# Clears of operand rings moved behind the first weight loads in a hybrid decoder layer

## The chip, the cores and the metric

The kernel runs on one core of a Trainium2 chip. The metric is device microseconds for one execution, as the median of several runs. The core has five engines with queues of their own, each worked off in order: TensorE (PE in the profile), VectorE (DVE), ScalarE (ACT), GpSimd (POOL) and SyncE (SP), which here only issues transfers. Engines wait for each other, and for transfers, by semaphores.

## The reference

One decoder layer over 1024 prompt tokens and 8 decode tokens, model width 1024, then a final norm. What is computed, cut to what matters here:

```
h = rmsnorm(x, norm1_g);  proj = h @ w_in            # 18 tiles of 128 columns
# columns 0..511: pooling mixer (windows 2, 4, 8, 16); columns 512..: RWKV-7
r, k, v, zw, za, zg = split(token_shift(proj[:, 512:]))
decay = exp(-exp(-softplus(-(w0 + tanh(zw) @ w_lora_up)) - 0.5))
a = sigmoid(a0 + za @ a_lora_up);  g = sigmoid(zg) @ g_lora_up
# per token and head: S = S * decay + (S @ -kk) (kk * a)^T + v k^T;  y = S @ r
x = x + concat(pool_out, rwkv_out) @ w_out
x = x + square(relu(rmsnorm(x, norm2_g) @ w_up)) @ w_down
y = rmsnorm(x, norm_f_g)
```

## The kernel before

All matrix products are done in three passes: an operand is split into a rounded half (`h`) and the rest (`l`), and `gemm` (L169 to L177) adds `h*h`, `h*l` and `l*h`. For a weight tile, `weights` (L147) loads `wr` over GpSimd's queue, ScalarE writes the rounded half `wh` (through `act`, L92) and VectorE the rest `wl` (L165). The ring of `wr` has four buffers. A tile of 128 output columns has two such loads of 256 KB, each with four of its eight 128-row pieces.

The start of the program is what matters here. `token_block(0)` and `token_block(1)` load the first two blocks of 256 tokens over SP's queue (`xr`, L213), round them (`xh` on ScalarE, `xl` on VectorE, L217), and sum their squares (`acc`, eight squares on ScalarE); a matmul with ones gives the sum over channels (`ss`, L239), and `rstd` (L130) makes the scale `rs` of it: `ms`, `tt`, `rs` on ScalarE, three steps on VectorE. Projection tiles 16 and 17 (`pj16`, `pj17`) come first: they hold the low-rank inputs `zw`, `za` and `zg`. `low_rank` (L305) scales them by `rs` (`pr`, L284), mixes in the shifted token (`z`) and takes the tanh and sigmoid in several steps on ScalarE and VectorE (`sigm`). Then `rkv` projects tiles 8, 4 and 12 (`pj8`, `pj4`, `pj12`) for the first head pair. A projection writes one of two shared PSUM buffers, and `pj17` two others, so the four blocks of `pj16` and `pj17` can be done before `rs` is known.

Later, `stage1` (L337) writes scaled operands into the buffers `ARs`, `RBs` and `BK`, of which half must be zero, and `inverse` (L455) writes the `TTs`. These buffers are cleared once. In the kernel before, `ARs`, `RBs` and `BK` are cleared on GpSimd where they are made (L434), and `TTs` on VectorE in `inverse_setup` (L445 to L453), which is called behind the first token blocks and the loads of weight tiles 16 and 17.

The order on each engine isn't that of the source: the framework's scheduler places each instruction by its priority, which follows the order of the source, and by its own estimate of when an operand is ready. `tc.high_priority` moves a step ahead. So the clears at L434, which stand ahead in the source, also stand ahead in GpSimd's queue.

Of the kernel before, what the change touches and what calls it, by code (L numbers as in the profile page):

```python
# [79 lines left out]
def build(nc, tc, I, O, dbg=None):  # L80
    with ExitStack() as ctx:
        _build(ctx, nc, tc, I, O, dbg or {})


def _build(ctx, nc, tc, I, O, dbg):
    V, A, PE, SY, GP = nc.vector, nc.scalar, nc.tensor, nc.sync, nc.gpsimd
# [342 lines left out]
    ARs = [rcp.tile([P, 4, 2, 2, 64], F32, name=f"AR{i}") for i in range(NSEG)]  # L429
    RBs = [rcp.tile([P, 4, 2, 64], F32, name=f"RB{i}") for i in range(NSEG)]  # L430
    BK = rcp.tile([P, 4, 4, 64], F32, name="BK")
    ring = [0]
    for t in (*ARs, *RBs, BK):
        GP.memset(t, 0.0)  # L434

# [2 lines left out]
    TTs = [rcp.tile([P, 8, 2, 64], F32, name=f"TT{i}") for i in range(2)]  # L440
# [4 lines left out]
    def inverse_setup():  # L445
        V.memset(Xs, 0.0)
        for t in range(16):
            V.memset(Xs[:, 17 * t:17 * t + 1], 1.0)
        V.memset(Es, 0.0)
        for t in TTs:  # L450
            V.memset(t, 0.0)
        for d in inv_d:
            SY.dma_start(d[:, :, 16:32, 32:64].rearrange("c g i k -> (c g) i k"), Es[0:32, :, 0:32])  # L453

# [331 lines left out]
    for w, r, src in ((wup, R[0], "w_lora_up"), (aup, R[1], "a_lora_up")):  # L786
# [4 lines left out]
        V.tensor_tensor(lol[r], raw[r], f32(w[r]), op=ALU.subtract)  # L791
    SY.dma_start(glu, I["g_lora_up"])
    inverse_setup()
    low_rank(0)

# [272 lines left out]
```

## Time and profile before

| | |
|---|---|
| median of 3 runs | 1366.24 us (1365.65 to 1368.66) |
| profiled execution | 1369.13 us, span 1367.4 us |
| TensorE busy | 1306.5 us, 96% |
| VectorE, ScalarE, GpSimd busy | 829.6, 592.7, 156.5 us |
| first matmul | 13.71 us after the span's start |

The profile shows one execution, with times from the start of its span. A row of the timeline gives the start, the duration, the engine, the line, the operation, and in brackets how long the engine had stood idle and what released it. Where several instructions are merged (x4), the duration is from the first one's start to the last one's end. The chain of waits follows the work that ended last back to the start of the program.

### The profile page before, as it was taken

The page shows a single profiled execution, that of the slowest core. Times are in us where ns is not written, and L with a number is a line of the kernel's source. Part 1 is how long each engine was busy: PE and PEld are TensorE (multiplying, and loading weights), DVE is VectorE, ACT ScalarE, POOL GpSimd, SP SyncE. Part 2 cuts the span into 40 slices and gives each one's busy share as a digit, 9 for nine tenths or more (in the row PEclk, how much of TensorE's full clock was granted, in tenths as well). Part 3 has the DMA queues.
Part 4 walks back from the last instruction along what each step waited for, and adds up shares of the span by engine and source line. Part 5 has one row for each costly group of instructions (what it writes and reads, how often), then busy time and mean ns, then how long its engine had stood idle before and what let it go on. Part 6 is the DMA issues. An engine that isn't in the chain of part 4 may idle for free.

```text
span 1367.4 us, 24591 instructions
## 1 busy us (share of the span) xinstructions
PE 1306.5 (96%) x9844; PEld 1158.8 (85%) x9844; DVE 829.6 (61%) x1832; ACT 592.7 (43%) x1466; POOL 156.5 (11%) x306
## 2 busy tenths in 40 slices
PE   5999999999999999999999999999999999999996
PEld 5987778788777777798999999999999999999986
DVE  8887677778778656748644435445444354453447
ACT  7768777877777758526211212112111121121123
POOL 4101000210010021120010100100000100000000
PEclk9999999899999989999999999999999999999998
DMA  6323123222221244531111111111111111111103
GB/s 199 97 55 89 39 47 83 100 96 54 59 63 42 67 152 147 167 125 59 47 54 39 55 47 39 55 40 47 55 40 54 47 46 48 45 48 48 47 7 124
DMA packets 75315, 94.82 MB, mean 69 GB/s; under 512 B 46168, under 2 KB 52440, under 8 KB 75192
## 3 DMA queue, kind: packets, MB, share of 16 engines
q0 software_dynamic: 20480, 66.04, 15.1%
q1 hardware_dynamic: 53392, 25.36, 7.1%
q10 hardware_dynamic: 1328, 1.85, 0.4%
q8 instruction: 77, 1.26, 0.4%
q14 instruction: 38, 0.31, 0.1%
HBM read 79.67 MB, written 13.78 MB: 68 GB/s over the span
## 4 chain that ended last, share of the span: by engine, by line
PE 75%; ACT 9%; DVE 9%; DMA 3%; issue 2%; POOL 1%; SPq 0%; DVEq 0%; POOLq 0%; ACTq 0%
PE dn L175 26%; PE up L175 26%; PE pj L175 7%; PE mx L175 5%; ACT SV L92 2%; DVE tm L496 1%; PE sc L403 1%; PE pcs L580 1%; ACT Es L92 1%; ACT TT L92 1%; PE pcs L577 1%; DVE SV L589 1%; ACT wh L92 1%; PE pcs L573 1%; PE bkt L417 1%
## 5 line engine op out<-in xcount | busy, mean ns | idle before, releaser
L92 ACT ACTIVATE wh<-wr 128x512 fp32r<-128x512 f32 x230 | 143.8, 626 | 353.4 <-PE dn L175 276.2
L175 PE MATMUL up<-h2h,wl 128*128 128x260 f32 (+1 forms) x768 | 245.8, 320 | 0.0
L175 PE MATMUL up<-h2h,wh 128*128 128x260 f32 (+1 forms) x768 | 245.2, 320 | 0.5 <-DVE u L910 0.5
L175 PE MATMUL up<-h2l,wh 128*128 128x260 f32 (+1 forms) x768 | 245.0, 320 | 0.0
L175 PE MATMUL dn<-uh,wl 128*128 128x512 f32 (+1 forms) x720 | 231.2, 321 | 0.0
L175 PE MATMUL dn<-ul,wh 128*128 128x512 f32 (+1 forms) x720 | 230.8, 321 | 0.0
L175 PE MATMUL dn<-uh,wh 128*128 128x512 f32 (+1 forms) x720 | 230.5, 320 | 0.0
L949 DVE TENSOR_TENSOR x<-dn,x 128x260 f32<-128x260 f32 (+1 forms) x192 | 99.1, 516 | 189.8 <-PE dn L175 189.8
L175 PE MATMUL pj<-xh,wh 128*128 128x256 f32 (+1 forms) x576 | 175.3, 304 | 13.9 <-ACT wh L92 13.7
L165 DVE TENSOR_TENSOR wl<-wr,wh 128x512 fp32r<-128x512 f32 x230 | 156.5, 684 | 44.6 <-ACT wh L92 37.8
L175 PE MATMUL pj<-xh,wl 128*128 128x256 f32 (+1 forms) x576 | 171.0, 297 | 0.2 <-DVE wl L165 0.2
L175 PE MATMUL pj<-xl,wh 128*128 128x256 f32 (+1 forms) x576 | 170.5, 296 | 0.0
L175 PEld LDWEIGHTS up<-h2l,wh 128*128 128x128 f32 x768 | 144.6, 188 | 12.1 <-DVE h2l L892 0.4
L175 PEld LDWEIGHTS up<-h2h,wh 128*128 128x128 f32 x768 | 144.3, 188 | 11.6 <-DVE u L910 0.9
L175 PEld LDWEIGHTS up<-h2h,wl 128*128 128x128 f32 x768 | 144.6, 188 | 11.0
L92 ACT ACTIVATE uh<-u 128x260 fp32r<-128x260 f32 (+1 forms) x96 | 47.2, 492 | 238.6 <-DVE u L911 238.6
L175 PEld LDWEIGHTS dn<-ul,wh 128*128 128x128 f32 x720 | 135.6, 188 | 10.9 <-issue 0.2
L175 PEld LDWEIGHTS dn<-uh,wh 128*128 128x128 f32 x720 | 135.8, 189 | 10.4
L175 PEld LDWEIGHTS dn<-uh,wl 128*128 128x128 f32 x720 | 135.5, 188 | 10.6 <-issue 0.2
L175 PEld LDWEIGHTS pj<-xh,wh 128*128 128x128 f32 x576 | 111.4, 193 | 17.4 <-ACT wh L92 13.7
L910 DVE SCALAR_TENSOR_TENSOR u<-up,rs 128x260 f32<-128x260 f32 (+1 forms) x96 | 49.5, 517 | 120.9 <-PE up L175 114.3
L175 PEld LDWEIGHTS pj<-xl,wh 128*128 128x128 f32 x576 | 111.2, 193 | 2.4 <-issue 1.9
(295 smaller groups left out, 2224.3 us busy)
## 6 DMA issues: line engine op xcount, KB each, us to landing
wr<-in_w_in POOLq DMA_DIRECT2D x72, 256.0 KB, 3.1
wr<-in_w_up POOLq DMA_DIRECT2D x64, 256.0 KB, 2.8
wr<-in_w_down POOLq DMA_DIRECT2D x64, 256.0 KB, 2.9
wr<-in_w_out POOLq DMA_DIRECT2D x26, 256.0 KB, 3.1
xr<-in_xT SPq DMA_DIRECT2D x16, 256.0 KB, 3.7
mr<-mix SPq DMA_DIRECT2D x8, 260.0 KB, 3.5
x<-in_xT SPq DMA_DIRECT2D x2, 1040.0 KB, 9.1
blk<-AA SPq DMA_DIRECT2D x16, 128.0 KB, 3.3
```

Source lines behind the costliest of these rows:

```text
L92: A.activation(out, in_, func, bias=bias, scale=scale, **k)
L165: V.tensor_tensor(l[:, :w], raw[:, :w], f32(h[:, :w]), op=ALU.subtract)
L175: PE.matmul(ps, lhs, rhs, start=i == 0, stop=i == n - 1)
L403: PE.matmul(psc[:, c, :], BK[:, c, 2 * h:2 * h + 2, :], AR[:, c, :, h, :], start=True, stop=True)
L417: PE.transpose(pt[:, c, :], BK[:, c, 2 * h:2 * h + 2, :].rearrange("p a t -> p (a t)"), ident)
L496: V.tensor_tensor(pr[:, q], l[:, q].unsqueeze(2).to_broadcast([64, m, m, m]), r[:, q].rearrange("p k j -> p j k").unsqueeze(1).to_broadcas ...
L573: PE.matmul(pq, AR[:, c, 0, :, :], SV[:, c, :, :], start=True, stop=True)
L577: PE.matmul(pa, TT[:, g, :, :], Q, start=True, stop=True)
L580: PE.matmul(pu, BKT[:, c, :, :], SV[:, c, :, :], start=True, stop=True)
L589: V.scalar_tensor_tensor(dst, pu[R[h], h, :], U.gam[R[h], g:g + 1], sg[R[h], h, :], ALU.mult, ALU.add)
L910: V.scalar_tensor_tensor(u, ps[:, :n], 0.0, rs2[:, cs], ALU.max, ALU.mult)
L949: V.tensor_tensor(d, ps[:, :n], d, op=ALU.add)
```

## The change

The clears of `ARs`, `RBs` and `BK` are taken from where the buffers are made and put into `inverse_setup`, together with those of the two `TTs`, which move from VectorE to GpSimd. Nothing else in the source differs.

```diff
     BK = rcp.tile([P, 4, 4, 64], F32, name="BK")
     ring = [0]
-    for t in (*ARs, *RBs, BK):
-        GP.memset(t, 0.0)
...
         V.memset(Es, 0.0)
-        for t in TTs:
-            V.memset(t, 0.0)
+        for t in (BK, *ARs, *RBs, *TTs):
+            GP.memset(t, 0.0)
         for d in inv_d:
```

GpSimd's queue in the kernel before, from the last two of its nine clears (`wr` is a weight load; `SV` and `AA` are two small clears of the first head pair):

```order
L434 MEMSET RB_145 128x512
L434 MEMSET BK 128x1024
L157 DMA wr<-in_w_in 128x512 x4
L559 MEMSET SV_0_743 64x64 x2
L342 MEMSET AA_0_679 128x16
```

The same queue in the changed kernel, from the last of the framework's own constants:

```order
L1036 MEMSET const-uint8-127 128x1
L1040 UNCONDITIONAL_BRANCH
L157 DMA wr<-in_w_in 128x512 x4
L449 MEMSET BK 128x1024
L449 MEMSET AR_138 128x1024
```

The four loads of weight tiles 16 and 17 now stand at the head of the queue, and eleven clears behind them.

ScalarE's first steps in the kernel before (`xh0` is the rounded half of the first token block, two steps for each loaded `xr0`):

```order
L100 ACT_TABLE_LOAD
L92 ACTIVATE xh0_172<-xr0_0_176,vec_87 128x256 x2
L92 ACTIVATE xh0_172<-xr0_2_182,vec_87 128x256 x2
L92 ACTIVATE xh0_172<-xr0_4_194,vec_87 128x256 x2
L92 ACTIVATE xh0_172<-xr0_6_200,vec_87 128x256 x2
```

and in the changed kernel:

```order
L100 ACT_TABLE_LOAD
L92 ACTIVATE wh_159<-wr_157 128x512
L92 ACTIVATE xh0_163<-xr0_0_167,vec_87 128x256 x2
L92 ACTIVATE xh0_163<-xr0_2_173,vec_87 128x256 x2
L92 ACTIVATE wh_181<-wr_179 128x512
L92 ACTIVATE xh0_163<-xr0_4_185,vec_87 128x256 x2
```

The rounding of the first weight tile's two halves, which came behind 15 of the 16 roundings of `x`, now stands first and sixth.

ScalarE in the low-rank block of the kernel before. `z00` and `z10` are the two low-rank tiles of the first half of the tokens, `pr12` and `pr13` the scaled projections, `za0` a rounded half; `wh_461` and `wh_467` are the two halves of weight tile 8, for `pj8`, the projection behind `pj17`:

```order
L92 ACTIVATE z00_317<-pr12_1_376,ona_94 128x256
L92 ACTIVATE z10_320<-pr13_0_407,ona_94 128x256
L92 ACTIVATE carry_127<-pr13_0_407 128x1
L92 ACTIVATE wh_461<-wr_459 128x512
L92 ACTIVATE carry_127<-pr12_1_376 128x1
L92 ACTIVATE z00_317<-z00_317 64x512
L92 ACTIVATE za0_319<-z00_317 64x512
L92 ACTIVATE wh_467<-wr_465 128x512
```

The same place in the changed kernel, up to two steps behind `wh_461` (one more `z10` step and then `wh_467` follow):

```order
L92 ACTIVATE carry_127<-pr13_0_407 128x1
L92 ACTIVATE z10_320<-pr13_1_437,ona_94 128x256
L92 ACTIVATE carry_127<-pr12_1_376 128x1
L92 ACTIVATE z00_317<-z00_317 64x512
L92 ACTIVATE za0_319<-z00_317 64x512
L92 ACTIVATE carry_127<-pr13_1_437 128x1
L92 ACTIVATE z00_317<-z00_317 64x512
L92 ACTIVATE z10_320<-z10_320 128x512
L92 ACTIVATE z00_317<-z00_317 64x512
L92 ACTIVATE wh_461<-wr_459 128x512
L92 ACTIVATE z10_320<-z10_320 128x512
L92 ACTIVATE zw0_318<-z00_317 64x512
```

Between the `carry` of `pr13_0` and `wh_461` there was nothing; now eight steps of the low-rank block stand there. Ahead of these rows, the rounding `aup` of the second lora weight has moved from ahead of `ms` of the first token block to behind it. On TensorE the order differs only up to the end of `pj8` (16 rows), where in the kernel before four matmuls of its second token block stand within the first; behind that TensorE, and a little later the other engines too, have the same order in both kernels.

## Rows read from the trace of the kernel before

**Rows 1.** The page's busy times, their share of the span and instruction counts.
```profile
PE 1306.5 (96%) x9844; PEld 1158.8 (85%) x9844; DVE 829.6 (61%) x1832; ACT 592.7 (43%) x1466; POOL 156.5 (11%) x306
```
**Rows 2.** Chain of waits, 0 to 50 us: start us, us, what.
```profile
7.09 5.91 DMA wr<-in_w_in
...
13.71 7.62 PE pj L175 x42
...
29.21 0.70 DVE wl L165
...
29.95 17.29 PE pj L175 x142
```
**Rows 3.** Timeline of GpSimd, first 8 us: start us, us, what.
```profile
0.74 3.67 POOL L434 MEMSET AR<- 128x1024 f32 x4 [0.29 <-POOLq L1038]
4.35 1.91 POOL L434 MEMSET RB<- 128x512 f32 x4
6.20 0.96 POOL L434 MEMSET BK<- 128x1024 f32 x1
7.09 2.29 POOL L157 DMA_DIRECT2D wr<-in_w_in  x4
```
**Rows 4.** Tile views of wr (0 to 40 us) and of xr (0 to 25).
```profile
DMA to landing us min/median/max: 2.8/3.3/6.5
...
DMA to landing us min/median/max: 2.7/4.4/5.2
```
**Rows 5.** Busy by stretch (PE, PEld, DVE, ACT, POOL), PEclk, DMA share, GB/s.
```profile
1.00:2.00 1.00, 0.00 (x0) 0.00 (x0) 0.89 (x2) 1.00 (x1) 1.00 (x2) 1.00 0.15 32
...
10.00:13.00 3.00, 0.00 (x0) 0.00 (x0) 1.22 (x4) 0.70 (x2) 0.43 (x1) 1.00 1.03 373
```
**Rows 6.** Timeline of ScalarE, 0 to 33 us.
```profile
6.21 4.50 ACT L92 ACTIVATE xh<-xr,vec 128x256 fp32r<-128x256 f32 x11 [0.52 <-DMA xr<-in_xT]
...
18.24 1.66 ACT L92 ACTIVATE xr<-xr 128x512 f32<-128x512 f32 x3
...
22.23 0.48 ACT L92 ACTIVATE ms<-ss,sm 128x256 f32<-128x256 f32 x1 [0.70 <-PE ss L239]
...
28.56 0.62 ACT L92 ACTIVATE wh<-wr 128x512 fp32r<-128x512 f32 x1
...
29.17 0.62 ACT L92 ACTIVATE z<-z 64x512 f32<-64x512 f32 x1
29.82 0.63 ACT L92 ACTIVATE za<-z 64x512 fp32r<-64x512 f32 x1
30.47 0.63 ACT L92 ACTIVATE wh<-wr 128x512 fp32r<-128x512 f32 x1
```
**Rows 7.** Timeline of VectorE, 0 to 52 us.
```profile
2.46 1.03 DVE L125 TENSOR_SCALAR ona<-vec 128x14 f32<-128x14 f32 x1 [0.24 <-DMA vec<-in_vecs]
...
4.53 1.68 DVE L217 SCALAR_TENSOR_TENSOR xl<-xr,vec,xh 128x256 fp32r<-128x256 f32 x4
6.75 4.48 DVE L217 SCALAR_TENSOR_TENSOR xl<-xr,vec,xh 128x256 fp32r<-128x256 f32 x11 [0.54 <-ACT xh L92]
...
16.18 0.91 DVE L451 MEMSET TT<- 128x1024 f32 x1 [0.16 <-issue]
...
31.32 0.69 DVE L165 TENSOR_TENSOR wl<-wr,wh 128x512 fp32r<-128x512 f32 x1
```
**Rows 8.** Timeline of TensorE, 18 to 20 us.
```profile
18.44 0.42 PE L175 MATMUL pj<-xh,wl 128*128 128x256 f32 x1
18.66 0.42 PE L175 MATMUL pj<-xh,wh 128*128 128x256 f32 x1
...
19.03 0.28 PE L175 MATMUL pj<-xh,wl 128*128 128x256 f32 x1
```
**Rows 9.** TensorE by stretch: busy us (matmuls), granted clock, DMA share, GB/s.
```profile
234.00:237.40 3.40, 2.20 (x91) 1.00 0.51 171
237.40:240.80 3.40, 3.40 (x45) 0.50 0.02 5
```

## The prediction

> **What bounds the kernel now.** I read the page's engine rows first: TensorE is busy for 96% of the span [rows 1], so a change pays only where TensorE stands still, or where it is made to. Then the chain of waits over the first 50 us [rows 2]: until 13.71 us it isn't on TensorE at all. GpSimd clears nine buffers [rows 3], issues the first weight load at 7.09, the load lands 5.91 us later, ScalarE rounds it, and only then does the first projection start. From 13.71 to 47.24 TensorE is all but continuous (7.62 us of matmuls, the square sums, then 142 matmuls in 17.29 us [rows 2]). One more view decides this case: what ScalarE does between 22 and 33 us [rows 6], because the chain comes back to it, through the `wl` at 29.21 [rows 2], just when TensorE has run out of prepared work: its matmul with that `wl` starts at 29.95, 0.04 us after the `wl` is done.
>
> **The change, step by step.**
>
> *The first four weight loads* move from 7.09 to where the clears began, 0.74 [rows 3]: 6.35 us earlier. How long will one take there? The trace has no weight load at the start. Loads of this size landed 2.8 us after issue at best and 6.5 at worst [rows 4]; the DMA engines are nearly idle from 1 to 2 us and full from 10 to 13, when the first load took 5.91 [rows 2, 5]. An issue at 0.74 is nearest to the idle case, so I take a landing at 3.6 and keep 6.65 (0.74 plus 5.91) for the range. TensorE could start at about 4.8, after one rounding of a weight tile and one of `x`: 8.9 us earlier than now.
>
> *What that buys at the first norm.* The next joint is ScalarE's first step on the square sum (`ms`, 22.23 [rows 6]). Ahead of it stand four weight roundings, 16 roundings of `x` (eleven in 4.50 us, so 0.41 each), eight squares (three in 1.66, 0.55 each) and one more rounding: 4 x 0.55 + 16 x 0.41 + 9 x 0.55, about 13.7 us [rows 6]. From 3.6 that ends at 17.3 if ScalarE is never starved. It will be: the 1 MB of the four weight loads now goes over the same DMA engines as the 2 MB of `x`. The `x` loads landed 2.7 to 5.2 us after issue [rows 4], the last at about 9.9; 1 MB more at the 373 GB/s of a full stretch [rows 5] is 2.8 us, of which a part falls into the idle start; I take 1.9, so the last `x` tile at 11.8, its roundings done by 12.8, then two weight tiles, the squares and the lora rounding: `ms` at 18.7, with 17.3 and 19.5 as ends. That is 3.5 us earlier than 22.23, not 6.35, because ScalarE used to do its roundings of `x` while the weights were on their way.
>
> *What eats it.* TensorE has the four blocks of `pj16` and `pj17` (96 matmuls) to do; starting at 4.8, paced by ScalarE until about 13.5 and then at full rate, it is through by about 21. Everything behind them is `pj8`, which needs the rounding of the next weight tile, `wh_461`. In the kernel before, that stood 28.56 - 22.23 = 6.33 us behind `ms` [rows 6]. In the changed order eight more ScalarE steps of the low-rank block stand ahead of it, and the rounding of `aup` has moved behind `ms`. Their prices: two 64x512 steps at 0.65 each (29.17 to 29.82 to 30.47), three more of that width at 0.55, one of 256 columns at 0.41, two of one column at about 0.1, and 0.55 for `aup` [rows 6]; together 4.1 us. So `wh_461` starts at 18.7 + 6.33 + 4.1 = 29.1 against 28.56: 0.5 us later, with ends of 0.9 earlier (17.3) and 1.3 later (19.5). The 3.5 us are spent, and TensorE stands idle from 21 to about 29.7.
>
> *After that.* The second half of that tile (`wh_467`) comes three ScalarE steps behind the first (0.55 + 0.65 + 0.55, after the 0.55 of `wh_461`): start 31.4, and `wl` 1.2 us behind, ended 32.6 or so; before, it ended at 32.01 (31.32 + 0.69 [rows 7]). That is 0.6 later. The kernel before had 18 of `pj8`'s 48 matmuls done when it needed that `wl`, the changed order has 15: 3 x 0.12, 0.35 us more.
>
> *The clock.* In its first 5 us TensorE's matmuls stand 0.22 us apart and take 0.42 (18.44, 18.66); at 19.03 one takes 0.28 [rows 8], and in the warm stretch they are 0.12 apart (17.29 / 142 [rows 2]). From 234.0 to 237.4 it was busy for 2.20 of 3.40 us, and the next stretch has a granted clock of 0.50, 1.2 GHz in place of 2.4 [rows 9]. An idle stretch of 8 us will do the same: the 15 matmuls behind 29.7 then take 3.2 us, which the wait until 32.6 hides; what remains is the time from 32.6 until the clock is back. At the start it took from 13.71 to about 18.9; the stretch at half clock shown in rows 9 is 3.4 long. So the clock is back 3.4 to 5.2 us behind 29.7, at 33.1 to 34.9: 0.5 to 2.3 us at half rate, cost 0.2 to 1.2; I take 0.6.
>
> *The other edits, at nothing.* The two `TT` clears leave VectorE (0.91 each [rows 7]); VectorE waits for ScalarE all through this stretch, so nothing is won there. On GpSimd the eleven clears (3.67 + 1.91 + 0.96 and two of 0.91 [rows 3, 7], 8.4 us) now run from 3.0 to 11.4, ahead of two small clears, the copy of `state_pool` and the fifth weight load. That load must wait for its ring slot, freed by the third `wl` at about 14, so the clears are covered by 2 us; without that cover they would delay a tile that isn't used before 29. The cleared buffers are first used far behind, in the first unit's `stage1` and `inverse`. On SP's queue the lora loads now stand ahead of `glu` and the two stores from `Es`, and land well before their use at 18.
>
> **Sum**: 0.6 + 0.35 + 0.6 = 1.55, say 1.6 us slower, with ends of 0.2 faster (0.9 earlier, + 0.35 + 0.3) and 2.9 slower (1.3 + 0.1 + 0.35 + 1.2). Behind 33 us both kernels have the same order on TensorE, which is then busy to 47 and beyond, so a shift passes through unchanged. The profiled execution took 1369.13 us (span 1367.4), 2.9 above the median of the runs: 1370.7 by its own scale, 1367.8 by the median.
>
> **A rule against the change.** Four small VectorE steps from 2.46 on, of up to 14 columns, each last until about 3.5 [rows 7], which is when GpSimd's third clear ends: VectorE was held by a clear. But `xl` steps during the clears come 0.42 apart (four in 1.68), and 0.41 later (eleven in 4.48), so these were not held. The Trainium skill, SBUF — State Buffer, section "Who interferes with whom", says that GpSimd and VectorE share a port pair under an exclusive lock, where the loser waits for the whole instruction, and that steps with two SBUF inputs meet only GpSimd steps that read SBUF. By its first half alone the clears would hold all of VectorE; by its second, and by the trace, not the `xl` and `wl` steps, and the sum stands.
>
> **Rivals.**
> 1. *The start gain partly survives*: ScalarE isn't starved and `ms` comes at 17.3 or a little before. For: ScalarE idled only 0.5 us between `x` tiles before. Against: 1 MB more goes through the same DMA engines. It gives 0.2 faster: 1366.0. To be faster by over 0.2% the low-rank steps would also have to run without their present waits for VectorE; I see no row for that, and give it a small chance.
> 2. *ScalarE blocked at its head* (slower): its first step is now the rounding of the first weight tile, with all of `x` queued behind. If that load takes 5.91 us again, ScalarE starts at 6.65 in place of about 3.6, and since it then waits no more for `x`, `ms` comes at 6.65 + 13.7, 20.4 or so, 1.7 behind the forecast; the sum is 1.6 + 1.7 = 3.3 slower: 1369.5. It decides from a landing at about 5.5. Against: at 0.74 nothing else is on the way.
> 3. *VectorE shut out by the clears* from 3.0 to 11.4: its 16 `xl` and four `wl` steps (16 x 0.41 + 4 x 0.6, 9 us) would begin at 11.4, the square sums would be ready at about 23, and the sum is some 6 slower: 1372. The `xl` spacing speaks against it.
> 4. *The clock stays up*: 1.0 slower: 1367.2. Rows 9 speak against it.
>
> **How the numbers follow.** Forecast 0.58; rival 1 0.18; rival 2 0.16; rival 3 0.03; rival 4 0.05. 0.2% is 2.7 us, about what a measurement of this kernel tells from no change. Slower by that: rival 2 for the most part, rival 3, and the top of the forecast's range (0.1): 0.28. Faster by that: half of rival 1: 0.09. Within: 0.63. The range takes in rival 2 and the lower end with 1 us for the scatter of the runs: 1364.8 to 1370.7.
>
> **What would show it.** In the changed kernel's timeline: the first weight load at about 0.7, landed by 3.6; the first matmul at about 5; `ms` at 18 to 19.5; then TensorE idle for some 8 us until about 29.5, its wait ended by the rounding of `wh`, and matmuls 0.21 apart behind it. Wrong would be: no such gap; a first rounding later than 5.5 (rival 2); `xl` steps 0.9 apart (rival 3).

## The result, and the profile after

The changed kernel takes 1376.64 us, the median of four runs (1374.20 to 1380.75), against 1365.95 for the kernel before on the same chip: 1.0079 of it, 95% interval 1.006 to 1.0098, or 10.7 us slower. A second comparison gave 1.0059 (1.0038 to 1.0081), 8 us by that ratio and 10.1 by the medians (1378.01 against 1367.93). The forecast was 1367.8, with 1364.8 to 1370.7 as its range: the sign was right, the size was not. The profiled execution took 1374.92 us.

The page's engine rows: busy us, share of the span, instructions. They answer [rows 1] and say nothing of the cause.

```profile
PE 1305.2 (95%) x9844; PEld 1156.8 (84%) x9844; DVE 836.7 (61%) x1830; ACT 592.6 (43%) x1466; POOL 158.3 (12%) x308
```

The chain of waits over the first 60 us: start us, us, what.

```profile
1.25 3.67 DMA wr<-in_w_in
...
6.21 6.74 DVE xl L217
12.99 10.95 PE pj L175 x75
...
35.19 0.53 ACT wh L92
35.76 19.64 PE pj L175 x144
```

Against [rows 2]: the first weight load does come 5.8 us earlier, and the first matmul starts at 6.02 instead of 13.71. But the second has to wait for an `xl` that takes 6.74 us where it took 0.4, and the 144 matmuls that stand before the first step of the low-rank product (`pw`) end at 55.40, where the kernel before was at 47.24: 8.2 us later. That difference then passes through: the first store of `AA` to memory (`blk`) stands at 78.92 in the chain and stood at 70.74. The spans of the two profiled executions are only 5.7 us apart (1373.1 and 1367.4), because behind that store the one shown here is 2.5 us shorter: in two stretches of 33 and 50 us, around 250 and 510 us, its mean granted clock is 0.90 and 0.93, where the kernel before had 0.84 and 0.86. The two comparisons, with more runs, don't show such a gain.

The timeline of GpSimd, first 14 us, and of VectorE, 1 to 24 us: start us, us, engine, line, operation; in brackets the idle time before and what ended it. From L430 on, line numbers are 2 lower than before.

```profile
1.25 2.29 POOL L157 DMA_DIRECT2D wr<-in_w_in  x4 [0.80 <-POOLq L1036]
3.50 0.99 POOL L449 MEMSET BK<- 128x1024 f32 x1
4.39 3.67 POOL L449 MEMSET AR<- 128x1024 f32 x4
7.96 1.97 POOL L449 MEMSET RB<- 128x512 f32 x4
9.83 1.89 POOL L449 MEMSET TT<- 128x1024 f32 x2
11.62 0.39 POOL L557 MEMSET SV<- 64x64 f32 x2
```

```profile
2.57 0.17 DVE L125 TENSOR_SCALAR ona<-vec 128x14 f32<-128x14 f32 x1 [0.37 <-DMA vec<-in_vecs]
2.66 9.18 DVE L126 TENSOR_SCALAR ona<-vec 128x4 f32<-128x4 f32 x1
...
5.60 6.94 DVE L165 TENSOR_TENSOR wl<-wr,wh 128x512 fp32r<-128x512 f32 x1
6.21 6.73 DVE L217 SCALAR_TENSOR_TENSOR xl<-xr,vec,xh 128x256 fp32r<-128x256 f32 x1
...
11.85 2.27 DVE L217 SCALAR_TENSOR_TENSOR xl<-xr,vec,xh 128x256 fp32r<-128x256 f32 x3
```

This is where the time is lost. The step at L126 makes four columns of constants (1 minus a gain, 128x4 numbers) and lasts 9.18 us; the two small steps behind it (L127, L128) last nearly as long, and the one ahead of it (L125) takes 0.17. The step at L126 ends at 11.84, just behind the first of the two `SV` clears, which is the last step of a run of clears that follow each other without a gap; the second `SV` clear waits for the first. The first `wl` (5.60) and the first `xl` (6.21) stand behind it in VectorE's queue and look long for that reason alone. The hold begins ahead of the first clear's row: L126 starts at 2.66, while GpSimd still issues loads, and `BK` at 3.50. In the kernel before, all four steps were held too, but for 1.0 us [rows 7].

ScalarE's timeline and, under it, TensorE by stretch (busy us with matmul count for PE, PEld, then DVE, ACT, POOL; granted clock; DMA share, GB/s):

```profile
4.94 0.63 ACT L92 ACTIVATE wh<-wr 128x512 fp32r<-128x512 f32 x1 [2.92 <-DMA wr<-in_w_in]
...
9.51 4.90 ACT L92 ACTIVATE xh<-xr,vec 128x256 fp32r<-128x256 f32 x12 [1.83 <-DMA xr<-in_xT]
...
24.84 0.48 ACT L92 ACTIVATE ms<-ss,sm 128x256 f32<-128x256 f32 x1 [4.18 <-PE ss L239]
...
35.10 0.61 ACT L92 ACTIVATE wh<-wr 128x512 fp32r<-128x512 f32 x1
```

```profile
27.90:35.76 7.86, 0.13 (x2) 0.00 (x0) 6.82 (x23) 6.10 (x17) 0.63 (x3) 0.68 0.15 50
35.76:40.89 5.13, 5.13 (x23) 5.12 (x24) 3.91 (x6) 3.70 (x7) 2.15 (x4) 0.50 0.31 100
40.89:55.41 14.52, 14.52 (x124) 14.42 (x122) 8.70 (x19) 7.57 (x18) 3.22 (x6) 1.00 0.46 146
```

`ms`, which the forecast put at 18.7, came at 24.84, later even than before (22.23 [rows 6]); `wh_461` follows 10.26 us behind it. TensorE stands idle for 7.9 us until then, and its next 23 matmuls run at a granted clock of 0.50, the lower of its two levels (1.2 GHz), 0.22 us each against 0.12 in the stretch behind. One row of the tile view of `xr`, 0 to 25 us, answers [rows 4]:

```profile
DMA to landing us min/median/max: 2.9/7.6/8.2
```

The tokens land much later than before (4.4 in the median).

### The profile page after: what moved, and what is told of

It reads as the page before. It is cut to its first block, busy times and chain, and to the rows that moved or that the text cites. A ratio compares the mean times of both kernels' runs of the same rounds, so it can differ in the third digit from the quotient of the medians.

```text
span 1373.1 us, 24596 instructions
## 1 busy us (share of the span) xinstructions
PE 1305.2 (95%) x9844; PEld 1156.8 (84%) x9844; DVE 836.7 (61%) x1830; ACT 592.6 (43%) x1466; POOL 158.3 (12%) x308
## 4 chain that ended last, share of the span: by engine, by line
PE 76%; ACT 10%; DVE 8%; DMA 3%; issue 2%; SPq 0%; POOL 0%; DVEq 0%; POOLq 0%; ACTq 0%
PE dn L175 26%; PE up L175 26%; PE pj L175 8%; PE mx L175 5%; ACT SV L92 2%; DVE tm L494 1%; PE pcs L578 1%; PE sc L403 1%; ACT TT L92 1%; ACT Es L92 1%; PE pcs L575 1%; PE pcs L571 1%; ACT wh L92 1%; PE bkt L417 1%; DVE SV L587 1%
## 5 line engine op out<-in xcount | busy, mean ns | idle before, releaser
L165 DVE TENSOR_TENSOR wl<-wr,wh 128x512 fp32r<-128x512 f32 x230 | 164.6, 724 | 42.8 <-ACT wh L92 35.6
L175 PEld LDWEIGHTS up<-h2h,wh 128*128 128x128 f32 x768 | 144.1, 188 | 11.7 <-DVE u L908 0.9
```

Source lines behind the costliest of these rows:

```text
L165: V.tensor_tensor(l[:, :w], raw[:, :w], f32(h[:, :w]), op=ALU.subtract)
L175: PE.matmul(ps, lhs, rhs, start=i == 0, stop=i == n - 1)
```

## The experiments

Theory H: a small VectorE step is held through GpSimd's run of clears, and all of VectorE's queue stands behind it. Rival P: clears hold every VectorE step. Rival Q: VectorE waited for something else. Rival 2 of the prediction, ScalarE blocked at its head, is out already: its first rounding starts at 4.94, below the 5.5 from which that rival decides.

### The held steps on another engine

```diff
-    V.tensor_scalar(omu, vec[:, V_MU:V_MU + 14], -1.0, 1.0, ALU.mult, ALU.add)
+    act(omu, vec[:, V_MU:V_MU + 14], AF.Identity, bias=1.0, scale=-1.0)
...                                        # oka, nw0, na0 likewise
```

> The changed kernel with one edit: the four small constants made from vec (1-mu, 1-ka, -w0, -a0) are computed on ScalarE instead of by the four VectorE steps at the head of its queue; the eleven clears on GpSimd stay where they are. Theory H (only those four steps are held by the run of clears, and everything else on VectorE stands behind them in order): the xl steps run at their own pace from about 5.5 us, ms starts near 18.7 to 19.5 us instead of 24.84, and the time falls by 6 to 8 us, to 1368 to 1370. Rival P (the clears hold every VectorE step, whatever it is): the first xl still ends after 11.8 us, ms near 24.8, time about 1376. Rival Q (VectorE waited for something that has nothing to do with the clears, a load or a semaphore): the wait moves to ScalarE, whose first steps then end near 11.8 us, and the time stays at 1375 to 1377.

VectorE and ScalarE of this run:

```profile
6.14 1.67 DVE L217 SCALAR_TENSOR_TENSOR xl<-xr,vec,xh 128x256 fp32r<-128x256 f32 x4
...
9.91 4.88 DVE L217 SCALAR_TENSOR_TENSOR xl<-xr,vec,xh 128x256 fp32r<-128x256 f32 x12 [1.49 <-ACT xh L92]
```

```profile
9.37 4.90 ACT L92 ACTIVATE xh<-xr,vec 128x256 fp32r<-128x256 f32 x12 [1.74 <-DMA xr<-in_xT]
...
20.42 0.48 ACT L92 ACTIVATE ms<-ss,sm 128x256 f32<-128x256 f32 x1 [0.42 <-PE ss L239]
...
30.70 0.61 ACT L92 ACTIVATE wh<-wr 128x512 fp32r<-128x512 f32 x1
```

and its tile view of `xr`, 0 to 25 us:

```profile
DMA to landing us min/median/max: 2.8/7.4/8.1
```

1.002 of the kernel before (1.0004 to 1.0036), about 2.7 us slower by that ratio (the medians are 3.9 us apart). The clears run as in the changed kernel, from 3.5 to 11.7, and `xl` steps run through them at 0.41 each: P is out, and so is Q, since ScalarE made the constants at 2.53 without any wait but that for `vec`. `ms` moves from 24.84 to 20.42. The expectation's time of 1368 to 1370 was met less closely than its direction (1371.64, on a chip where the kernel before had 1367.74); `ms` is 0.9 to 1.7 us later than it said, of which more below. The same edit in the kernel before, as a control, and the changed kernel itself once more:

> The kernel before with the four constants on ScalarE instead of VectorE: the control for the variant of the changed kernel with the same edit. There the constants wait 1.0 us and VectorE is not what the first rounding waits for, so nothing should move: ms within 0.5 us of 22.23, ratio 0.999 to 1.001. If the edit itself costs or brings time, this shows it.

> The changed kernel as it is, beside the others of this set, so that the size of its loss is known from more runs and on the chip on which its variants run. Expected from the front of the trace: 4.4 us behind the variant with the constants on ScalarE (its first matmul of the third weight tile starts at 35.76 us against 31.36 us there), so 1.005 to 1.009 of the kernel before. If the loss of the first comparison were mostly chance in the clock, it would come out at 1.001 to 1.004.

1.0004 (0.9987 to 1.0021) with `ms` at 21.82, so the edit by itself is worth nothing that these runs can tell; and 1.0059 (1.0038 to 1.0081) for the changed kernel, as expected. There all four constants were held:

```profile
2.64 9.20 DVE L125 TENSOR_SCALAR ona<-vec 128x14 f32<-128x14 f32 x1 [0.44 <-DMA vec<-in_vecs]
```

### The length of the run of clears

One kernel clears nine of the eleven buffers twice in a row, one puts the two `TT` clears back on VectorE:

```diff
-        for t in (BK, *ARs, *RBs, *TTs):
+        for t in (BK, *ARs, *RBs, BK, *ARs, *RBs, *TTs):
```

> The changed kernel with nine of the eleven clears (BK, ARs, RBs) issued twice in a row, about 6.5 us more of clears without a gap. Theories H and P: the three VectorE constants end with the last clear, near 18.3 us instead of 11.85, ms starts near 31.3 us instead of 24.84, and the time is about 6.5 us above the changed kernel's, 1382 to 1384. Rival Q: the constants still end near 11.85 us and the time stays within 1 us of the changed kernel's. (The order of some later wh steps on ScalarE differs by a few places, which may move the time by a microsecond or so.)

> One part of the change undone: the two TT clears go back to VectorE, nine clears stay on GpSimd behind the loads of the first weights. Theories H and P: the run of clears ends some 1.9 us earlier (near 9.9 us), the VectorE constants end there, ms starts near 23 to 24 us (the two clears of 0.9 us each now cost VectorE up to 1.8 us of its own time) and the time is 0 to 2 us below the changed kernel's, 1374.5 to 1376.5. Rival Q: constants still end near 11.85 us.

The held step of the first, then of the second:

```profile
2.63 15.55 DVE L126 TENSOR_SCALAR ona<-vec 128x4 f32<-128x4 f32 x1
```

```profile
2.84 7.21 DVE L126 TENSOR_SCALAR ona<-vec 128x4 f32<-128x4 f32 x1
```

They end at 18.18 and 10.05 us, where 18.3 and 9.9 were expected: the hold is as long as the run. The times fit less well. With the clears doubled `ms` came at 30.85, but the kernel took 1.0076 of before (1.0048 to 1.0104), no more than the changed kernel. In that order three weight roundings stand ahead of most of the low-rank block, so that of 6 us more at `ms` little is left where TensorE goes on (37.01, against 35.76); the first store of `AA` was at 76.43 in the chain, earlier than in the changed kernel. Where its remaining loss arises is not shown. With `TT` back, `ms` came at 25.55, no earlier than in the changed kernel and later than the 23 to 24 expected; 1.0065 (1.0045 to 1.0085). The order on TensorE had changed: 86 projection matmuls stand ahead of its first square sum, where the changed kernel has 76 and the kernel before had 42, and all but the first run without a gap. From the chain:

```profile
12.21 12.44 PE pj L175 x85
```

The square sum starts right behind them, at 24.48; VectorE's sums for it had ended by 23.9. So the ten matmuls take back 1.5 us (12.44 against 10.95) of what the shorter hold gave. Of the two clears on VectorE only the first, ahead of the first `xl`, can have cost `ms` anything, at most its 0.9 us.

### A gap, or no run at all

In the first of these kernels the raw tiles of the low-rank weights take other buffers, so that weight tile 8 can be asked for early; GpSimd then issues a load behind the clear of `BK` which has to wait for the first `wl`. In the second GpSimd must wait for the constants before its first clear.

```diff
+    ahead[8] = weights(I["w_in"][8])
...
-        raw = wp.tile([P, 512], F32, tag="wr", name=f"r{src}", bufs=NWR)
+        raw = s1.tile([P, 520], F32, tag="kr"[len(up)], name=f"r{src}", bufs=NRKV)[:, :512]
```

> The changed kernel with the VectorE constants left where they are, but with gaps in the run of clears: the two raw tiles of the low-rank weights take other buffers and weight tile 8 is asked for before the low-rank block, so that GpSimd, behind the clear of BK, issues a weight load that has to wait for VectorE's first wl. Theory H with the addition that any gap lets VectorE in: the constants end at about 4.6 us, right behind the clear of BK, and GpSimd goes on with its clears only after the first wl, near 6 to 8 us; ms near 19 to 20 us. As the first half of tile 8 is then rounded ahead of the low-rank block, TensorE's idle stretch of 8 us should shrink by most of its length too: time 1358 to 1366. Rival P (every VectorE step is held by clears): xl steps after the first gap are again held until the run ends, near 14 us. Rival Q: constants still end near 11.85 us, time above 1370.

```diff
+    gate = cp.tile([P, 1], F32, name="gate")
+    V.tensor_scalar(gate, na0[:, 0:1], -1.0, None, ALU.mult)
...
+        GP.memset(gate, 0.0)
         for t in (BK, *ARs, *RBs, *TTs):
```

> The changed kernel with the four constants left on VectorE, and one step more: before its first clear GpSimd clears a single column that VectorE has written behind the constants, so that the run of clears cannot begin before the constants are made. Theory H (it is the run of clears that holds the constants, and nothing else in the change): the constants end by 3.7 us, clears run from about 3.8 to 12.1 us beside the xl steps without holding them, ms at 20.3 to 20.9 us, as with the constants on ScalarE, and the time is that variant's, 1.001 to 1.004 of the kernel before. Rival (the loads issued on GpSimd hold them too, or xl is held by clears): ms above 22 us.

The constants in the first kernel, with the clear that held them, and in the second:

```profile
2.71 1.83 DVE L126 TENSOR_SCALAR ona<-vec 128x4 f32<-128x4 f32 x1
```

```profile
3.51 0.99 POOL L449 MEMSET BK<- 128x1024 f32 x1
6.78 0.54 POOL L157 DMA_DIRECT2D wr<-in_w_in  x1 [2.29 <-DVE wl L165]
```

```profile
2.56 0.16 DVE L126 TENSOR_SCALAR ona<-vec 128x4 f32<-128x4 f32 x1
...
6.20 1.67 DVE L219 SCALAR_TENSOR_TENSOR xl<-xr,vec,xh 128x256 fp32r<-128x256 f32 x4
```

With the gap they end at 4.5, right behind `BK`. With the gate they take 0.16 to 0.29 us each beside the weight loads that GpSimd issues at that time (1.24 to 3.52). In the changed kernel the hold began beside the same loads, at 2.66, so the issuing of loads alone doesn't hold: it takes clears that GpSimd can go on to without a wait. When GpSimd takes from VectorE what these steps need, the start of a row doesn't show. `ms` is at 21.01, 0.1 above the range, and the time 1.0027 of before (1.0012 to 1.0041), as with the constants on ScalarE. Theory H stands, and one column takes the hold away; the rest of the changed kernel's loss stays. The kernel with the gap is faster than before, 0.9969 (0.9949 to 0.9989): with the first half of tile 8 rounded at 19.58, TensorE goes on at 25.83 in the chain, not at 35.76. With both remedies, and with the second alone in the kernel before:

> The changed kernel with both remedies: constants on ScalarE, and the raw tiles of the low-rank weights in other buffers, so that weight tile 8 is loaded and rounded ahead of the low-rank block. Against the variant that has only the second (constants held for 1.9 us, 0.9969 of the kernel before): its first wl came at 5.79 us and waited for the rounding, not for the constants, so that the constants cost nothing there: within 1 us of it, 1363 to 1367, 0.995 to 0.999 of before. If the constants still cost VectorE time there, it is 1 to 2 us faster than that.

> The kernel before with only the second remedy: the raw tiles of the low-rank weights in other buffers, weight tile 8 asked for ahead of the low-rank block; clears and weight loads as before. The loads of tile 8 then wait for the first wl, at 16 us, and land near 20 us; in ScalarE's order its rounding stands behind four steps of the low-rank block instead of behind seven. If what the variant with gaps gained (0.9969) came from tile 8 alone, this should gain as much, 1362 to 1365; if it takes the early weight loads too, this gains 0 to 2 us, 1366 to 1368.

0.9972 (0.9955 to 0.9988), the same as with the gap alone, as expected, and 1.0009 (0.9992 to 1.0026). The early request for tile 8 alone gains nothing: in the kernel before, tile 8's rounding came at 29.44, no earlier than its 28.56 without the edit.

### Who is let in

The row that the prediction went by [rows 7] seems to speak against theory H: in the kernel before, the same four steps got in after one clear, with clears behind it. So an extra step of that kind (128x4 numbers times -1) was put into the midst of the run, in the changed kernel with its constants on ScalarE, and in the kernel before (there of `xl`). These two kernels and the four behind them were each run once, for their traces:

```diff
+                V.tensor_scalar(probe[0], f32(l[:, 0:4]), -1.0, None, ALU.mult)
```

> The variant with the four constants on ScalarE, with one small VectorE step of the held kind put back (128 x 4 numbers of the first wl, times -1), but in another place: behind the first wl, so that VectorE comes to it at about 6.2 to 6.6 us, in the midst of the run of clears (3.5 to 11.7 us), and not ahead of it as in the changed kernel. Theory R (such a step is held until the run of clears has its first gap, wherever it comes in): it ends at 11.8 us, the xl behind it do too, ms near 24 to 25 us instead of 20.42. Theory S (only what stands at VectorE while GpSimd issues loads just ahead of the run is held through it; one that comes in between clears waits for the clear that runs, as in the kernel before, where the wait was 1.0 us): it ends by 7.6 us, ms at 20.4 to 21.5 us.

> The kernel before with one extra small VectorE step of the held kind (128 x 4 numbers of the second-finished xl, times -1) behind the first two xl steps, so that VectorE comes to it at about 5.2 to 5.5 us, in the midst of that kernel's own run of clears (0.74 to 7.16 us) and of the weight loads issued behind it (to 9.39 us). In the kernel before the four constants came to VectorE at 2.46 us and were let in after 1.0 us, with clears in front and behind. Theory U (clears in the kernel before let such a step in after the one that runs, for a reason that the changed kernel lacks): the extra step ends by 6.3 us. Theory V (they don't; the constants at 2.46 us were an exception): it is held past 7.1 us, to the first gap in GpSimd's queue at 9.55 us at the latest, and the xl behind it with it; ms may then come up to 1 us later than 22.23.

The extra step in the one and in the other:

```profile
6.86 4.98 DVE L170 TENSOR_SCALAR probe<-wl 128x4 f32<-128x4 f32 x1
```

```profile
5.52 0.30 DVE L222 TENSOR_SCALAR probe<-xl 128x4 f32<-128x4 f32 x1
```

Held to the end of the run in the one (to 11.84, and `ms` back at 23.76), let in behind the clear that ran in the other. Four more kernels vary what is around the clears: one weight load of the kernel before ahead of its clears; in the changed kernel the weight loads on SyncE's queue; that, with the clears in the order of before; and the kernel before with the weight loads on SyncE's queue.

> The kernel before with one of its four first weight loads issued on GpSimd ahead of its nine clears (the other three stay behind them). The constants come to VectorE at about 2.5 us, when the clears run from 1.9 to some 8.3 us. Theory W (a load issued on GpSimd ahead of a run of clears makes the run hold such steps to its end): they end at 8.3 us or later, up to the first gap in GpSimd's queue near 10.3 us. Rival X (it is the order or the place of the clears in the changed kernel): they are let in as in the kernel before, by 3.7 us.

> The variant with the constants on ScalarE and one extra small VectorE step in the midst of the run of clears, which was held for 5.0 us there, with the four first weight loads issued on SyncE's queue instead of GpSimd's, so that nothing but clears stands on GpSimd, from 0.74 to about 8.8 us. Theory W: the extra step is let in after one clear, its stay is under 1.1 us. Rival X: it is held to the end of the run, near 8.8 us (a stay of 2 to 3 us if it comes at 6 to 6.5 us).

> The variant with the constants on ScalarE, the extra small VectorE step behind the first wl and the first weight loads on SyncE's queue, in which the step was held for 3.1 us to the end of the run, with the clears in the order of the kernel before (ARs, RBs, BK, TTs instead of BK, ARs, RBs, TTs). If the order of the clears does it: the step ends within one clear, by 7 us. If not: it is held to the end of the run again, near 8.9 us.

> The kernel before with its extra small VectorE step behind the first two xl, and with the four first weight loads on SyncE's queue, so that they land during the run of clears (0.74 to 7.1 us) instead of behind it; the clears are as in the kernel before. If weights that land during the clears are what makes the run hold such steps: the four constants or the extra step (at about 6 us) end at 7.1 us or later. If it is the order or place of the clears: constants end by 3.6 us and the extra step within one clear.

In this order, the constants of the first and the extra step of the other three:

```profile
2.64 5.72 DVE L126 TENSOR_SCALAR ona<-vec 128x4 f32<-128x4 f32 x1
```

```profile
5.91 3.11 DVE L170 TENSOR_SCALAR probe<-wl 128x4 f32<-128x4 f32 x1
```

```profile
6.16 2.85 DVE L170 TENSOR_SCALAR probe<-wl 128x4 f32<-128x4 f32 x1
```

```profile
6.48 0.80 DVE L222 TENSOR_SCALAR probe<-xl 128x4 f32<-128x4 f32 x1
```

One load ahead of them, and the clears of the kernel before hold the constants to 8.35, the end of `BK`. But a load ahead isn't needed: with all of them on SyncE the extra step is still held, to 9.0, in either order of the clears (in the order of before it came in only at the ninth of eleven), so theory W of the expectations falls as the only cause, and so does the order. In the last kernel the constants got in at 3.5 as in the kernel before; the extra step was not let in behind `BK`, the clear that ran, and ended in the first gap of the run (7.28). So a step of this kind may get in between two clears, and did where the prediction had seen it; in seven kernels, the changed one among them, it didn't, over up to twenty clears. What decides it stays open.

### The loads moved, the clears left alone

The last two kernels issue the first four weight loads on SyncE's queue, among the tokens and in the order of need: one the changed kernel with both remedies, the other the kernel before without any other edit.

```diff
-    ahead[16] = weights(I["w_in"][16, :, 0:512])
+    ahead[16] = weights(I["w_in"][16, :, 0:512], q=SY)
...                                        # the second half of tile 16, and tile 17, likewise
```

> The changed kernel with the constants on ScalarE, the four first weight loads on SyncE's queue in the order in which they are needed (tile 17's behind the tokens), and the raw tiles of the low-rank weights in other buffers. If early weights and an undisturbed VectorE are what counts, its first rounding starts near 4.5 us and ms near 18 to 20 us, and it is as fast as the variant with both remedies or up to 2 us faster, 0.995 to 0.998 of the kernel before; but the first half of tile 8 is rounded behind the first step of the low-rank block and the second half later, which may give up 2 to 4 us of that: 0.998 to 1.001.

> The kernel before with one edit: the four loads of the first two weight tiles are issued on SyncE's queue among the tokens, in the order in which they are needed, instead of on GpSimd behind the clears. The clears stay at the head of GpSimd's queue, the constants on VectorE. From the look at the same kernel with an extra step (ms at 20.17 us, rounding of tile 8 at 23.67 us instead of 28.56 us, first step of the low-rank weights' product at 43.1 us instead of 47.24 us): 3 to 5 us faster than the kernel before, 1363 to 1366, 0.996 to 0.998. If early weights bring nothing without the rest, or cost the clock behind an idle stretch, as in the variants with weights first on GpSimd: 0.999 to 1.002.

The first is no faster than before, 1.0012 (0.9993 to 1.0032): tile 8's halves were rounded at 24.53 and 27.50, the second as late as the expectation feared. The second has the lowest ratio of all, 0.996 of before (0.9943 to 0.9977; 1363.28 us), though its interval doesn't tell it from the 0.9969 and 0.9972 above. ScalarE and, under it, the tile view of `xr`, 0 to 25 us:

```profile
19.48 0.48 ACT L92 ACTIVATE ms<-ss,sm 128x256 f32<-128x256 f32 x1
...
23.01 0.61 ACT L92 ACTIVATE wh<-wr 128x512 fp32r<-128x512 f32 x1
```

```profile
DMA to landing us min/median/max: 3.6/5.2/5.8
```

`wh_461` now stands 3.5 us behind `ms`, not 6.3: in ScalarE's order it comes ahead of the first step of the low-rank block (`z`). Its load is issued at 15.25, against 16.31 before, both times behind a wait for a `wl`; why the scheduler places the rounding earlier is not shown. This is what the change was after, got by moving four loads and no clear.

## Why the prediction was wrong

Its sum, term by term, against the traces. The variant with the constants on ScalarE shows what the change does without the hold.

- **The first weight load**: issue forecast at 0.74, landing at 3.6, first matmul at 4.8. Measured: issue at 1.25, landing at 4.92, first matmul at 6.02. Its 3.67 us from issue to landing are far from the 5.91 taken as the other end. Right in kind, 1.2 us late.
- **`ms` at 18.7, with 19.5 as the late end**: without the hold it comes at 20.42. The tokens are the main reason. Beside the weight loads their landing took 2.8, 7.4 and 8.1 us in that variant (least, median, most; 2.7, 4.4 and 5.2 before [rows 4]), so that the last `x` rounding ended at 14.27, not 12.8. The forecast had seen the contention and sized it too small: 1.7 us, of which this is 1.5.
- **Clears "covered", at nothing**: this is the step that failed, and with it the weighing of rival 3. The prediction saw that the four constants had been held by a clear. It then asked only whether `xl` and `wl` would be held themselves (they aren't), not who stands ahead of them in the same queue, and let the 1.0 us of one trace stand for how long such a step can be held. In place of nothing the runs showed 4.4 us, `ms` at 24.84 against 20.42.
- **`wh_461` 6.33 + 4.1 behind `ms`**: 10.26 in the changed kernel, 10.28 with the constants on ScalarE. Right.
- **TensorE idle for some 8 us, then half clock**: 7.9 us, and half clock up to 40.89, 5.1 us behind the restart, at the upper end of 3.4 to 5.2. The forecast let a wait for `wl_467` until 32.6 hide most of it, although by its own numbers the 15 matmuls ahead of that wait end at 29.7 + 3.2, 32.9; no such wait shows in the trace. From `wh_461` to the low-rank product it is 20.31 us (35.10 to 55.41), where the kernel before took 18.68 (28.56 to 47.24): 1.6 us more, where the sum had 1.05 (1.55 less the 0.5 by which `wh_461` itself was to be late). 0.6 us too little.

1.55 + 1.7 + 4.4 + 0.6 is 8.25 us; the low-rank product starts 8.2 us late, and the comparisons gave 10.7 us (8.2 to 13.4) and 8 us (5.2 to 11.1). The sum is at the low end of the first; whether more was lost in those runs is not shown. Without the hold, by the same sum, 3.9 us; the two kernels that take away nothing but the hold were 2.7 (0.5 to 4.9) and 3.7 us slower (1.6 to 5.6). So the mechanism on which the forecast was built is there, at about twice the size, and a second one of 4.4 us came on top. Rival 3 named the right engines, the right consequence ("some 6 slower: 1372") and the wrong victim: not the 16 `xl` steps but small steps for constants, in front of them in the queue. Its course is what the trace shows: `xl` and `wl` are done only from 11.85 on, where it had 11.4, and `ms` stands at 24.84, where it had the square sums at about 23. It was given a chance of 0.03, because `xl` steps aren't held by themselves.

The rule weighed there, the Trainium skill, SBUF — State Buffer, section "Who interferes with whom", bears on both kinds of step. It says that `tensor_scalar` may take the second port pair, which GpSimd also uses, and that steps with two inputs from SBUF meet only GpSimd steps that read. The runs agree: `TENSOR_SCALAR` steps were held by clears, `xl` and `wl` were not (0.41 and 0.69 us each in the midst of the run). The prediction had drawn on the section without what it says of `tensor_scalar`. The section's "for the whole instruction" doesn't cover what was measured, a hold over eleven instructions.

## What to carry to other kernels

Ask of every instruction that a move puts beside new work, the smallest first, what it is held by and what stands behind it in its queue: an in-order engine passes on the wait of a step of four columns to all that follows. A wait seen once, and short, is a sign that two steps exclude each other, not a measure of how long: bound it by the length of the whole run that it may meet. And if loads are wanted earlier, move the loads: on another queue, with the clears left where they were, they gave 0.996 (1.0012 in the one kernel that moved the clears too and asked for tile 8 early); ahead of the clears on the same queue, as the change had it, 1.006 to 1.008.

## What was not expected of the hardware

- Behind GpSimd's clears, one after the other, a VectorE step of 128x4 numbers lasted 9.18 us over eleven clears, and 15.55 us over twenty, of which 0.8 to 0.9 us lie ahead of the first clear's row; without them it took 0.16 us. In the kernel before, the same step got in after 1.0 us. Why it is let in there stays open.
- A step that waits so counts as busy. VectorE's busy time rose from 829.6 to 836.7 us, although two clears of 0.91 us were taken from it.
- 1 MB of weights loaded over one queue beside 2 MB of tokens over another took the tokens' median landing from 4.4 to 7.6 us. With both on one queue in the order of need it was 5.2 (the last kernel).
